# Gated DeltaNet layer of a two-layer trunk: later transfers of the block inverses in ScalarE's program, a pinned order of GpSimd's chain, and another PSUM rotation for two heads

## The chip, the cores and the metric

The kernel runs on one core of one Trainium2 chip. The metric is the device time of one execution in microseconds (us); the trace is that of one execution, recorded by the hardware profiler. Names of engines below: PE is TensorE (matmuls), ACT is ScalarE, DVE is VectorE, POOL is GpSimd, SP is the engine that issues most DMAs. Each of the five runs its own list of instructions strictly one after the other, and waits on semaphores for what the other engines produce. ACT also issues DMAs; such an issue stands in its list like any other instruction.

## The reference

The input is 512 tokens of width 1024. Two layers are computed, each as FFN (SwiGLU), mixer, FFN, all with residual adds. Layer 0 has an attention mixer, layer 1 a gated DeltaNet mixer with 8 heads of width 128. The change is in the second mixer only, which is in short (the reference uses chunks of 64 tokens, the kernel blocks of 128):

```python
q, k, v = silu(conv4(h @ w_in))            # per head; q and k are l2-normalized
beta, g = sigmoid(..), -exp(a_log) * softplus(..)
gc      = cumsum(g)                        # inside a chunk
l_mat   = strict_lower((k * beta) @ k.T * decay)
t_mat   = inverse(I + l_mat)               # triangular solve per chunk
u, w    = t_mat @ (v * beta), t_mat @ (k * beta * exp(gc))
a_qk    = lower(q @ k.T * decay)
for each chunk:                            # a scan over a 128 x 128 state
    v_new = u - w @ state
    o     = (q * exp(gc)) @ state + a_qk @ v_new
    state = state * exp(gc_last) + (k * exp(gc_last - gc)).T @ v_new
out = (rms_norm(o) * silu(gate)) @ w_out
```

## The kernel before

**Projections.** All large matmuls are done three times on rounded parts (high times high, low times high, high times low). A panel of weights comes by a DMA of SP into `raw`, ACT makes the high part `wh` (L174), DVE the low part `wl` (L175). One projection (queries, keys, values or gate of one pair of heads) fills two PSUM buffers `mm`, one for each head, with 96 matmuls of 0.23 us in two half panels. There are only these two `mm` buffers: the next projection starts when DVE has read the one before into `cx` (L926 in `gdn_conv`). A convolution of four taps follows: the first tap on ACT (`cy`, L929), three on DVE (`cy`, L931), an activation on ACT (`c`, L934 or L937), for most of the first two pairs' projections one more pass on DVE (`c`, L935).

**The delta rule.** Heads go in four pairs, 0 to 3. A pair passes through stages: `prep` (`gdn_keys`: transposes of k in PSUM buffers `pa`; row norms; `kdec` by ACT; then `pl`, the products k k^T, of which DVE makes `iu`, the matrix to be inverted; then q k^T, of which DVE makes `aq` in the tile `du`), `base` (`gdn_base`, below), `turned` (values turned and scaled, `vb`), `scan` (`gdn_head`, two heads side by side) and `gated`. Heads 0 and 1 are pair 0, heads 4 and 5 pair 2. PSUM has three buffers `pa` and three `pb`.

**`gdn_base`** inverts the 32x32 diagonal blocks of both heads of a pair at once. ACT issues two DMAs `iud<-iu` to DRAM and four `lb<-iud` back, which lay the blocks out over 128 partitions. POOL then runs a chain of 31 steps of two instructions each (`tmp<-rr,lb`, `rr<-rr,tmp`), 62 in all. After it ACT issues four DMAs `rd<-rr` to DRAM (L1043) and two `r<-rd` back (L1046), one for each head. In `gdn_head`, DVE transposes r into t (L1055), and PE begins the scan with `pb<-t,iu`. At its end DVE computes `a` from the output's squares (L1129), POOL raises it to the power -1/2 (`rs<-a`, L160), ACT scales the output by it (`on<-on,rs`, L1133), and PE transposes the output in `gated` (`pa<-ident,on`, L99).

**What sets the order.** `blend` runs one stream of projections (the filler: queries 0, values 0, keys 1, queries 1, values 1, gate 0, keys 2, queries 2, values 2, gate 1, out 0, keys 3, ..., out 2; a step is three matmuls) against the stages, by the table PLAN: a stage's first step and its pitch, both in filler steps. PE is held to the order in which this program is traced. On ACT, DVE and POOL a scheduler of the compiler orders the instructions, by its own estimate of times. `keep_in_program_order` (here `pin`) adds the constraint that an instruction comes behind the instruction of the same engine that was traced immediately before it. Each chain step of POOL is one step of its stage.

Of the kernel before, what the change touches and what calls it, by code (L numbers as in the profile page):

```python
# [13 lines left out]
ALU = mybir.AluOpType  # L14
# [21 lines left out]
QD = 5  # L36
NHID = 14
HDPAD, HIDPAD = 112, 0
TANH = ((0, 0), (2, 0), (1, 1), (0, 1))
PLAN = (  # L40
    ("setup", 0, 3.5, 5), ("decays", 0, 22, 0), ("prep", 0, 25.5, 2.1), ("turned", 0, 43.5, 1.82),
    ("base", 0, 51.5, 0.45), ("decays", 1, 47.5, 4.52), ("decays", 2, 57.5, 3.84),
    ("decays", 3, 50.5, 1.87), ("prep", 1, 82.5, 4.2), ("base", 1, 99.5, 0.41),
    ("scan", 0, 91.5, 1.91), ("turned", 1, 134.5, 1.09), ("gated", 0, 152.5, 1.33),
    ("scan", 1, 138.5, 2), ("prep", 2, 136.5, 3), ("base", 2, 151.5, 0.65),
    ("turned", 2, 192.5, 0.85), ("gated", 1, 188.5, 1.26), ("scan", 2, 202.5, 2.3),
    ("prep", 3, 209.5, 2.42), ("base", 3, 245.5, 0.47), ("turned", 3, 254.5, 0.85),
    ("gated", 2, 251.5, 0.73), ("scan", 3, 260.5, 0.95), ("gated", 3, 283.5, 1.22),
# [53 lines left out]
class Trunk:  # L102
# [610 lines left out]
    def odd_mixer(self, gain, w_in, conv, a_log, dt_bias, gnorm, w_out):  # L713
        nc = self.nc
        H = 8
        self.prenorm(gain)
        with ExitStack() as st:
            pool = st.enter_context(self.tc.tile_pool(name="gdn", bufs=2))
            one = st.enter_context(self.tc.tile_pool(name="gdn1", bufs=1))
            self.te = Ordered(self.tc)  # L720
            half = one.tile([P, 96], F32, name="half")
            nc.vector.tensor_scalar(half, conv, 0.5, None, ALU.mult)
            n = H // 2
            Ks = [[{}, {}] for _ in range(n)]
            keys, queries, values = (
                lambda p, sec=sec: self.gdn_proj(pool, Ks[p], sec, p, w_in, conv, half)
                for sec in (1, 0, 2))
            gate = lambda p: self.gdn_gate(pool, Ks[p], p, w_in)
            out = lambda p, mk=(self.mm_ps, self.mm_ps): self.gdn_out(Ks[p], p, w_out, mk)
            prep = lambda p: side_by_side(*(self.gdn_keys(pool, G, 2 * p + j, K)  # L730
                                            for j, K in enumerate(Ks[p])))
            base = lambda p: self.gdn_base(pool, G, Ks[p])
            turned = lambda p: (self.gdn_values(pool, K) for K in Ks[p])
            scan = lambda p: side_by_side(*(self.gdn_head(pool, G, 2 * p + j, K)
                                            for j, K in enumerate(Ks[p])))
            gated = lambda p: (self.gdn_gated(pool, K, gnorm) for K in Ks[p])
# [210 lines left out]
    def gdn_keys(self, pool, G, h, K):  # L947

        nc = self.nc
        S, big, v3, rep = self.gdn_tools(pool)
        du, kT, qT = G["du"][h], K["k"], K["q"]
        small = lambda tag: pool.tile([P, NB], F32, tag=tag, name=tag, bufs=4)
        pk = self.a_ps()
        for b in range(NB):
            self.te.transpose(out=pk[:, S[b]], in_=kT[:, S[b]], identity=self.ident)
        sk, br, kd = small("sk"), small("br"), small("kd")
        for b in range(NB):  # L960
            sq = pool.tile([P, P], F32, tag="gosq", name="gosq", bufs=1)
            nc.scalar.activation(sq, pk[:, S[b]], AF.Square, accum_out=sk[:, b:b + 1])
        nc.vector.tensor_scalar(sk, sk, 1e-6, None, ALU.add)
        nc.vector.reciprocal(br, sk)
        vs = small("vs")
        self.rpow(vs, sk, NB, 0.5)
        nc.vector.tensor_tensor(br, br, G["bt"][:, :, h], op=ALU.mult)
        nc.vector.tensor_tensor(kd, br, G["kdc"][:, :, h], op=ALU.mult)
        K["vs"] = vs
        kdec = big("kdec", bufs=4)  # L970
        for b in range(NB):
            nc.scalar.activation(kdec[:, S[b]], pk[:, S[b]], AF.Copy, scale=kd[:, b:b + 1])
# [12 lines left out]
        pq = self.b_ps()
        for b in range(NB):
            self.te.matmul(pq[:, S[b]], lhsT=kT[:, S[b]], rhs=qT[:, S[b]], start=b == 0, stop=b == 3)
        aq = du
        for b in range(NB):
            G["last"] = nc.vector.scalar_tensor_tensor(  # L990
                aq[:, S[b]], pq[:, S[b]], br[:, b:b + 1], du[:, S[b]], ALU.mult, ALU.mult)
        yield
        yield

        pn = self.a_ps()
        for b in range(NB):
            self.te.transpose(out=pn[:, S[b]], in_=qT[:, S[b]], identity=self.ident)
        sn = small("sn")
        for b in range(NB):
            sq = pool.tile([P, P], F32, tag="gosq", name="gosq", bufs=1)  # L1000
            nc.scalar.activation(sq, pn[:, S[b]], AF.Square, accum_out=sn[:, b:b + 1])
        eq = small("eq")
        nc.vector.tensor_scalar(eq, sn, P * EPS, 1e-6 * P * EPS, ALU.mult, ALU.add)
        K.update(aq=aq, eq=eq)
# [10 lines left out]
            nc.scalar.activation(vb[:, S[b]], pv[:, S[b]], AF.Copy, scale=K["vs"][:, b:b + 1])  # L1015
        K["vb"] = vb

    def gdn_base(self, pool, G, Ks):


        nc = self.nc
        n = BASE
        iud = self.dram.tile([2 * HPITCH], F32, tag="iud", name="iud", bufs=2)
        for j, K in enumerate(Ks):
            nc.scalar.dma_start(self.rows_of(iud, j), K["iu"].rearrange("p (t s) -> p t s", s=P))
        lb = pool.tile([P, n, n], F32, tag="lb", name="lb", bufs=1)
        rr = pool.tile([P, n // 4, n], F32, tag="rr", name="rr", bufs=1)
        tmp = pool.tile([P, 9 * n], F32, tag="tmp", name="tmp", bufs=1)
        quarters = [slice(q * 2 * NBLK, (q + 1) * 2 * NBLK) for q in range(4)]
        for s in quarters:  # L1030
            nc.scalar.dma_start(lb[s], self.blocks_of(iud))
        nc.scalar.copy(out=rr, in_=G["eye"])
        for j in range(n - 1):
            m, k = n - 1 - j, j // 4 + 1
            sh = [P, k, m]
            p = tmp[:, :k * m].rearrange("p (a b) -> p a b", b=m)
            nc.gpsimd.tensor_tensor(p, rr[:, :k, j:j + 1].broadcast_to(sh),  # L1037
                                    lb[:, j, j + 1:].rearrange("p (o m) -> p o m", o=1)
                                    .broadcast_to(sh), op=ALU.mult)
            nc.gpsimd.tensor_tensor(rr[:, :k, j + 1:], rr[:, :k, j + 1:], p, op=ALU.subtract)  # L1040
            yield
        for q, s in enumerate(quarters):
            nc.scalar.dma_start(self.blocks_of(G["rd"], q, 4), rr[s])  # L1043
        for j, K in enumerate(Ks):
            K["r"] = pool.tile([P, T], F32, tag="r", name="r", bufs=3)
            nc.scalar.dma_start(K["r"].rearrange("p (t s) -> p t s", s=P), self.rows_of(G["rd"], j))  # L1046
        yield
# [156 lines left out]
```

## Time and profile before

| what | us |
|---|---|
| three runs | 2032.43, 2032.97, 2032.87 |
| their median | 2032.87 |
| the profiled execution's own time | 2032.96 |
| span of its instructions | 2031.2 |
| PE busy in it | 1999.0 |
| DVE, ACT, POOL busy | 1084.6, 748.3, 130.9 |

The span is the time between the first and the last instruction; what lies around it is 1.8 us. A busy share says nothing yet of who waits for whom; that is read from the waits and from the order of rows on each engine.

### The profile page before, as it was taken

To read this page: it belongs to the slowest core of one execution; us is meant where nothing else is said; L and a number is where in the kernel's file an instruction comes from. 1 tells how busy PE (TensorE), PEld (TensorE's weight loads), DVE (VectorE), ACT (ScalarE), POOL (GpSimd) and SP (SyncE) were. 2 spreads that over 40 slices of the span, in tenths; PEclk is the share of its full clock that TensorE was granted. 3 is DMA by queue.
4 is the path that set the end of the run, shared out by engine and by line. 5 is a ranking of instruction groups with operands and counts; after the bars stand their busy time and mean duration, and the time that the engine had idled before them with its cause. 6 is when DMAs were issued, how large, how long until landed. Compare 5 with 4: busy or idle time off the path is not lost.

```text
span 2031.2 us, 24843 instructions
## 1 busy us (share of the span) xinstructions
PE 1999.0 (98%) x9786; PEld 1667.5 (82%) x9786; DVE 1084.6 (53%) x1752; ACT 748.3 (37%) x1359; POOL 130.9 (6%) x298
## 2 busy tenths in 40 slices
PE   8999999999999999999999999998999999999998
PEld 7888888889888888888888888877877788888887
DVE  6452454597675433444544344478577685443543
ACT  5232233355663222233332232355465453322322
POOL 0000000100000000000000000005432400000000
PEclk9999999999999999999999999999999999999999
DMA  4333333222123333333333333234223233223332
GB/s 157 94 99 98 94 99 98 86 84 73 47 90 103 94 104 94 94 103 94 94 95 102 94 95 103 93 111 115 77 80 92 75 100 104 94 90 97 93 101 76
DMA packets 189866, 192.24 MB, mean 95 GB/s; under 512 B 28546, under 2 KB 165044, under 8 KB 189748
## 3 DMA queue, kind: packets, MB, share of 16 engines
q1 hardware_dynamic: 158916, 182.62, 28.7%
q10 hardware_dynamic: 30832, 8.02, 1.7%
q8 instruction: 77, 1.26, 0.3%
q14 instruction: 41, 0.34, 0.1%
HBM read 185.35 MB, written 5.26 MB: 94 GB/s over the span
## 4 chain that ended last, share of the span: by engine, by line
PE 89%; POOL 5%; DMA 2%; DVE 1%; issue 1%; ACT 1%; ACTq 0%; SPq 0%; POOLq 0%
PE mm L181 10%; PE mm L182 10%; PE mm L183 10%; PE pa L181 9%; PE pa L183 8%; PE pa L182 8%; PE pb L181 8%; PE pb L183 8%; PE pb L182 8%; PE mm L96 4%; POOL tmp L1037 2%; POOL rr L1040 2%; PE pb L96 1%; DMA lb<-iud 1%; DMA iud<-iu 1%
## 5 line engine op out<-in xcount | busy, mean ns | idle before, releaser
L175 DVE TENSOR_TENSOR wl<-raw,wh 128x1024 fp32r<-128x1024 f32 (+1 forms) x348 | 413.2, 1187 | 564.1 <-ACT wh L174 563.1
L174 ACT CAST wh<-raw 128x1024 fp32r<-128x1024 f32 (+1 forms) x348 | 355.6, 1022 | 702.0 <-PE pb L182 279.9
L181 PE MATMUL mm<-xnh,wh 128*128 128x512 f32 (+1 forms) x816 | 316.5, 389 | 0.6 <-ACT wh L174 0.6
L183 PE MATMUL mm<-xnh,wl 128*128 128x512 f32 (+1 forms) x816 | 317.1, 389 | 0.0
L182 PE MATMUL mm<-xnl,wh 128*128 128x512 f32 (+1 forms) x816 | 316.7, 388 | 0.0
L181 PEld LDWEIGHTS mm<-xnh,wh 128*128 128x128 f32 x816 | 154.3, 189 | 31.6 <-ACT wh L174 1.0
L183 PEld LDWEIGHTS mm<-xnh,wl 128*128 128x128 f32 x816 | 154.2, 189 | 30.5 <-issue 0.5
L182 PEld LDWEIGHTS mm<-xnl,wh 128*128 128x128 f32 x816 | 154.3, 189 | 30.4 <-issue 0.2
L181 PE MATMUL pa<-xnh,wh 128*128 128x512 f32 x400 | 156.2, 390 | 0.0
L183 PE MATMUL pa<-xnh,wl 128*128 128x512 f32 x400 | 155.8, 389 | 0.0
L183 PE MATMUL pb<-xnh,wl 128*128 128x512 f32 x400 | 155.7, 389 | 0.0
L181 PE MATMUL pb<-xnh,wh 128*128 128x512 f32 x400 | 155.7, 389 | 0.0
L182 PE MATMUL pa<-xnl,wh 128*128 128x512 f32 x400 | 155.7, 389 | 0.0
L182 PE MATMUL pb<-xnl,wh 128*128 128x512 f32 x400 | 155.7, 389 | 0.0
L226 ACT CAST hid<-hd 128x512 fp32r<-128x512 f32 x88 | 54.5, 620 | 209.0 <-DVE hd L398 209.0
L96 PE MATMUL mm<-xnh,wh 128*128 128x512 f32 x256 | 109.2, 426 | 12.0 <-DVE cx L926 12.0
L392 DVE TENSOR_TENSOR gr<-mm,rb 128x512 f32<-128x512 f32 x80 | 55.2, 691 | 94.7 <-PE mm L183 94.6
L183 PE MATMUL pb<-hid,wl 128*128 128x512 f32 x264 | 102.8, 389 | 0.0
L181 PE MATMUL pa<-hid,wh 128*128 128x512 f32 x264 | 102.7, 389 | 0.0
L182 PE MATMUL pa<-hid,wh 128*128 128x512 f32 x264 | 102.7, 389 | 0.0
L183 PE MATMUL pa<-hid,wl 128*128 128x512 f32 x264 | 102.7, 389 | 0.0
L181 PE MATMUL pb<-hid,wh 128*128 128x512 f32 x264 | 102.7, 389 | 0.0
(308 smaller groups left out, 3365.1 us busy)
## 6 DMA issues: line engine op xcount, KB each, us to landing
raw<-in_ffn_w_gate_dram SPq DMA_DIRECT2D x88, 512.0 KB, 3.6
raw<-in_ffn_w_up_dram SPq DMA_DIRECT2D x88, 512.0 KB, 3.6
raw<-in_ffn_w_down_dram SPq DMA_DIRECT2D x88, 512.0 KB, 3.6
raw<-in_gdn_w_in_dram SPq DMA_DIRECT2D x32, 512.0 KB, 3.9
raw<-in_att_w_in_dram SPq DMA_DIRECT2D x24, 512.0 KB, 3.5
raw<-in_gdn_w_out_dram SPq DMA_DIRECT2D x16, 256.0 KB, 2.7
xr<-in_x_dram SPq DMA_DIRECT2D x4, 512.0 KB, 5.6
raw<-in_att_w_out_dram SPq DMA_DIRECT2D x4, 512.0 KB, 3.4
```

The lines of the kernel that those rows point to most:

```text
L96: return self.tc.keep_in_program_order(self.engine.matmul(*args, **kw))
L174: nc.scalar.copy(out=h[:, :n], in_=raw[:, :n])
L175: nc.vector.tensor_tensor(l[:, :n], raw[:, :n], h[:, :n].bitcast(F32), op=ALU.subtract)
L181: self.te.matmul(out, lhsT=lh, rhs=rh, start=start, stop=False)
L182: self.te.matmul(out, lhsT=lh, rhs=rl, start=False, stop=False)
L183: self.te.matmul(out, lhsT=ll, rhs=rh, start=False, stop=stop)
L226: nc.scalar.copy(out=h, in_=src)
L392: nc.vector.tensor_tensor(gr, g[j], self.rb, op=ALU.mult)
L1037: nc.gpsimd.tensor_tensor(p, rr[:, :k, j:j + 1].broadcast_to(sh), lb[:, j, j + 1:].rearrange("p (o m) -> p o m", o=1) .broadcast_to(sh), o ...
L1040: nc.gpsimd.tensor_tensor(rr[:, :k, j + 1:], rr[:, :k, j + 1:], p, op=ALU.subtract)
```

## The change

Four edits. First, 36 empty steps (50 for pair 1, none for pairs 2 and 3) stand between the chain's last step and the issues `rd<-rr`, and those issues are pinned. Second, both instructions of each chain step on POOL are pinned. Third, `pl` of heads 0 and 1 takes a buffer `pb` instead of `pa`. Fourth, PLAN starts scans 0 and 1 three filler steps later.

```diff
+WAIT = 36, 50, 0, 0
 PLAN = (
...
-    ("scan", 0, 91.5, 1.91), ("turned", 1, 134.5, 1.09), ("gated", 0, 152.5, 1.33),
-    ("scan", 1, 138.5, 2), ("prep", 2, 136.5, 3), ("base", 2, 151.5, 0.65),
+    ("scan", 0, 94.5, 1.91), ("turned", 1, 134.5, 1.09), ("gated", 0, 152.5, 1.33),
+    ("scan", 1, 141.5, 2), ("prep", 2, 136.5, 3), ("base", 2, 151.5, 0.65),
...
-        pl = self.a_ps()
+        pl = self.b_ps() if h < 2 else self.a_ps()
...
-            nc.gpsimd.tensor_tensor(rr[:, :k, j + 1:], rr[:, :k, j + 1:], p, op=ALU.subtract)
+            pin(nc.gpsimd.tensor_tensor(p, rr[:, :k, j:j + 1].broadcast_to(sh),
+                                        lb[:, j, j + 1:].rearrange("p (o m) -> p o m", o=1)
+                                        .broadcast_to(sh), op=ALU.mult))
+            pin(nc.gpsimd.tensor_tensor(rr[:, :k, j + 1:], rr[:, :k, j + 1:], p, op=ALU.subtract))
             yield
+        yield from [None] * wait
         for q, s in enumerate(quarters):
-            nc.scalar.dma_start(self.blocks_of(G["rd"], q, 4), rr[s])
+            pin(nc.scalar.dma_start(self.blocks_of(G["rd"], q, 4), rr[s]))
```

The compiled programs show where instructions move. Line numbers of the changed kernel are higher by one to two. The first place is POOL's list in the chain of pair 3 (`rr_13054`); `rs_13070` and `rs_13078` belong to the two heads of pair 2, and `vs` to pair 3's values. Before, the chain begins, and ends, like this:

```order
L160 TENSOR_TENSOR vs_12664<-sk_12651,halfTrue_89 128x4
L1037 TENSOR_TENSOR tmp_13055<-rr_13054,lb_13053 128x31
L1040 TENSOR_TENSOR rr_13054<-rr_13054,tmp_13055 128x31
L1037 TENSOR_TENSOR tmp_13055<-rr_13054,lb_13053 128x30
...
L1037 TENSOR_TENSOR tmp_13055<-rr_13054,lb_13053 128x16
L160 TENSOR_TENSOR rs_13070<-a2_13068,halfFalse_87 128x4
L1040 TENSOR_TENSOR rr_13054<-rr_13054,tmp_13055 128x8x2
L160 TENSOR_TENSOR rs_13078<-a2_13076,halfFalse_87 128x4
L1037 TENSOR_TENSOR tmp_13055<-rr_13054,lb_13053 128x8
```

In the changed program the same chain begins like this:

```order
L161 TENSOR_TENSOR vs_12664<-sk_12651,halfTrue_89 128x4
L1038 TENSOR_TENSOR tmp_13055<-rr_13054,lb_13053 128x31
L1041 TENSOR_TENSOR rr_13054<-rr_13054,tmp_13055 128x31
L1038 TENSOR_TENSOR tmp_13055<-rr_13054,lb_13053 128x30
L1041 TENSOR_TENSOR rr_13054<-rr_13054,tmp_13055 128x30
L161 TENSOR_TENSOR rs_13070<-a2_13068,halfFalse_87 128x4
L161 TENSOR_TENSOR rs_13078<-a2_13076,halfFalse_87 128x4
L1038 TENSOR_TENSOR tmp_13055<-rr_13054,lb_13053 128x29
```

Both `rs` of pair 2 moved from the chain's end to a place behind its second step: 58 chain instructions now stand behind them. Elsewhere POOL's list is as before.

The second place is ACT's list around `rd<-rr` of pair 0. `c_10842` and `c_10853` are pair 1's queries, `cx_10933` and `cx_10943` (changed: `cx_10925`) pair 1's values. Before:

```order
L929 ACTIVATE cy_10848<-cx_10845,half_10034 128x512
L174 CAST wh_11041<-raw_11039 128x1024
L934 ACTIVATE c_10842<-cy_10837 128x512
L1043 DMA rd_10279<-rr_10687 32x8x32 x4
L929 ACTIVATE cy_10936<-cx_10933,conv_248 128x512
L934 ACTIVATE c_10853<-cy_10848 128x512
L174 CAST wh_11161<-raw_11159 128x1024
L1046 DMA r_10881<-rd_10279 128x4x128
```

In the changed program:

```order
L930 ACTIVATE cy_10837<-cx_10834,half_10034 128x512
L175 CAST wh_10949<-raw_10947 128x1024
L1045 DMA rd_10279<-rr_10687 32x8x32 x3
L930 ACTIVATE cy_10848<-cx_10845,half_10034 128x512
L1045 DMA rd_10279<-rr_10687 32x8x32
L935 ACTIVATE c_10842<-cy_10837 128x512
L1048 DMA r_10963<-rd_10279 128x4x128
...
L175 CAST wh_11041<-raw_11039 128x1024
L935 ACTIVATE c_10853<-cy_10848 128x512
```

Against the projections' work, the first `rd` issues moved forward: they stand ahead of `cy_10848`, `c_10842` and the cast `wh_11041`, behind which they stood. For pair 1 they moved back, from a place ahead of the values' `cy` to one behind all eight `on<-on,rs` of pair 0.

The third place is DVE's list at the end of pair 1's values, where t is made from r of pair 0 and `cx` empties the two buffers `mm`. Before:

```order
L926 TENSOR_TENSOR cx_10933<-mm_10856,rb_10133 128x512
L931 SCALAR_TENSOR_TENSOR cy_10848<-cx_10845,half_10034,cy_10848 128x512
...
L931 SCALAR_TENSOR_TENSOR cy_10936<-cx_10933,conv_248,cy_10936 128x512
L926 TENSOR_TENSOR cx_10943<-mm_10857,rb_10133 128x512
...
L175 TENSOR_TENSOR wl_11162<-raw_11159,wh_11161 128x1024
L1055 STREAM_TRANSPOSE t_11057<-r_10881 128x512
```

In the changed program:

```order
L1057 STREAM_TRANSPOSE t_11066<-r_10963 128x512
L932 SCALAR_TENSOR_TENSOR cy_10848<-cx_10845,half_10034,cy_10848 128x512
L176 TENSOR_TENSOR wl_11042<-raw_11039,wh_11041 128x1024
L926 MEMSET cx_10935 128x3
L936 SCALAR_TENSOR_TENSOR c_10853<-c_10853,cy_10848 128x512
L1057 STREAM_TRANSPOSE t_11068<-r_10965 128x512
L927 TENSOR_TENSOR cx_10925<-mm_10856,rb_10133 128x512
L932 SCALAR_TENSOR_TENSOR cy_10928<-cx_10925,conv_248,cy_10928 128x512
L927 TENSOR_TENSOR cx_10935<-mm_10857,rb_10133 128x512
```

Both transposes moved ahead of the two `cx`, behind which they stood.

## Rows read from the trace of the kernel before

**Rows 1.** The page, first part: busy time, share of span, instructions.

```profile
PE 1999.0 (98%) x9786; PEld 1667.5 (82%) x9786; DVE 1084.6 (53%) x1752; ACT 748.3 (37%) x1359; POOL 130.9 (6%) x298
```

**Rows 2.** Waits of PE in the second mixer: us in total, times, longest.

```profile
PE mm L96 <- DVE cx L926: 12.0, 3, 6.5
```

**Rows 3.** Busy time per 50 us stretch; behind the engines granted clock, DMA share, GB/s.

```profile
1400.00:1450.00 50.00, 43.00 (x303) 35.71 (x302) 29.69 (x70) 22.17 (x62) 19.19 (x48) 0.93 0.38 98
```

**Rows 4.** Timeline of PE: start, duration, instruction, idle time before and its releaser.

```profile
1368.61 1.16 PE L96 MATMUL pa<-c 128*128 128x128 f32 x8 [2.56 <-ACT kdec L972]
...
1386.90 0.39 PE L96 MATMUL mm<-xnh,wh 128*128 128x512 f32 x1
...
1406.92 0.39 PE L96 MATMUL mm<-xnh,wh 128*128 128x512 f32 x1
...
1417.20 0.80 PE L96 MATMUL mm<-xnh,wh 128*128 128x512 f32 x1 [6.49 <-DVE cx L926]
...
1422.36 0.40 PE L96 MATMUL mm<-xnh,wh 128*128 128x512 f32 x1
...
1475.59 0.80 PE L96 MATMUL mm<-xnh,wh 128*128 128x512 f32 x1 [4.82 <-DVE cx L926]
...
1479.60 0.91 PE L99 MATMUL pa<-ident,c 128*128 128x128 f32 x4
...
1605.88 1.35 PE L99 MATMUL pa<-ident,on 128*128 128x128 f32 x4 [2.54 <-ACT on L1133]
...
1616.70 0.89 PE L96 MATMUL pb<-t,iu 32*32 32x32 f32 x32
```

**Rows 5.** Timeline of ACT around the transfers of pairs 0 and 1.

```profile
1413.12 1.82 ACTq L1043 DMA_DIRECT2D rd<-rr  x4
1415.04 0.72 ACT L929 ACTIVATE cy<-cx,conv 128x512 f32<-128x512 f32 x1 [11.99 <-issue]
...
1470.39 1.81 ACTq L1043 DMA_DIRECT2D rd<-rr  x4
```

**Rows 6.** Timeline of DVE at the places that the change reorders.

```profile
1370.47 0.74 DVE L931 SCALAR_TENSOR_TENSOR cy<-cx,half,cy 128x512 f32<-128x512 f32 x1
...
1385.17 0.68 DVE L926 TENSOR_TENSOR cx<-mm,rb 128x512 f32<-128x512 f32 x1
...
1416.46 0.68 DVE L926 TENSOR_TENSOR cx<-mm,rb 128x512 f32<-128x512 f32 x1
1417.06 0.68 DVE L935 SCALAR_TENSOR_TENSOR c<-c,cy 128x512 f32<-128x512 f32 x1
1417.66 0.75 DVE L931 SCALAR_TENSOR_TENSOR cy<-cx,conv,cy 128x512 f32<-128x512 f32 x1
1418.32 1.22 DVE L175 TENSOR_TENSOR wl<-raw,wh 128x1024 fp32r<-128x1024 f32 x1
1419.46 0.70 DVE L1055 STREAM_TRANSPOSE t<-r 128x512 f32<-128x512 f32 x1
...
1599.91 0.15 DVE L1129 SCALAR_TENSOR_TENSOR a<-gss,eq 128x4 f32<-128x4 f32 x1
```

**Rows 7.** Timeline of POOL: chain of pair 0, chain of pair 3.

```profile
1381.34 0.24 POOL L1037 TENSOR_TENSOR tmp<-rr,lb 128x31 f32<-128x31 f32 x1 [14.08 <-DMA lb<-iud]
...
1412.88 0.21 POOL L1040 TENSOR_TENSOR rr<-rr,tmp 128x8 f32<-128x8 f32 x1
...
1579.70 0.56 POOL L1037 TENSOR_TENSOR tmp<-rr,lb 128x31 f32<-128x31 f32 x1 [14.28 <-DMA lb<-iud]
...
1581.85 0.57 POOL L1037 TENSOR_TENSOR tmp<-rr,lb 128x29 f32<-128x29 f32 x1
...
1604.38 1.01 POOL L160 TENSOR_TENSOR rs<-a,halfFalse 128x4 f32<-128x4 f32 x1
1605.36 0.22 POOL L1040 TENSOR_TENSOR rr<-rr,tmp 128x16 f32<-128x16 f32 x1
...
1606.80 0.21 POOL L1040 TENSOR_TENSOR rr<-rr,tmp 128x8 f32<-128x8 f32 x1
```

More of the change, by code (lines that the diff above doesn't have):

```diff
@@ L731, in odd_mixer @@
                                             for j, K in enumerate(Ks[p])))
-            base = lambda p: self.gdn_base(pool, G, Ks[p])
+            base = lambda p: self.gdn_base(pool, G, Ks[p], WAIT[p])
             turned = lambda p: (self.gdn_values(pool, K) for K in Ks[p])
@@ L1016, in gdn_values, with gdn_base @@
         K["vb"] = vb
-    def gdn_base(self, pool, G, Ks):
-        nc = self.nc
+    def gdn_base(self, pool, G, Ks, wait):
+        nc, pin = self.nc, self.tc.keep_in_program_order
         n = BASE
@@ L1036, in gdn_base @@
             p = tmp[:, :k * m].rearrange("p (a b) -> p a b", b=m)
-            nc.gpsimd.tensor_tensor(p, rr[:, :k, j:j + 1].broadcast_to(sh),
-                                    lb[:, j, j + 1:].rearrange("p (o m) -> p o m", o=1)
-                                    .broadcast_to(sh), op=ALU.mult)
-            nc.gpsimd.tensor_tensor(rr[:, :k, j + 1:], rr[:, :k, j + 1:], p, op=ALU.subtract)
+            pin(nc.gpsimd.tensor_tensor(p, rr[:, :k, j:j + 1].broadcast_to(sh),
+                                        lb[:, j, j + 1:].rearrange("p (o m) -> p o m", o=1)
+                                        .broadcast_to(sh), op=ALU.mult))
+            pin(nc.gpsimd.tensor_tensor(rr[:, :k, j + 1:], rr[:, :k, j + 1:], p, op=ALU.subtract))
             yield
+        yield from [None] * wait
         for q, s in enumerate(quarters):
-            nc.scalar.dma_start(self.blocks_of(G["rd"], q, 4), rr[s])
+            pin(nc.scalar.dma_start(self.blocks_of(G["rd"], q, 4), rr[s]))
         for j, K in enumerate(Ks):
```

## The prediction

> **What bounds the kernel now.** I first read the page's busy times: PE works 98% of the span [rows 1], so time can only come or go where PE stands idle or runs slowly. Next I read what PE waits for in the second mixer [rows 2]: 12.0 us in all for `cx`. PE's timeline [rows 4] has the single waits: 2.56 us for `kdec`, because `pl` wants a buffer `pa`; 6.49 and 4.82 for `cx`; 2.54 for `on`. Behind the last three, matmuls of one weight panel start 0.43 us apart rather than 0.23 us; in the stretch that holds the first one the granted clock is 0.93 on average [rows 3], so part of it ran at the lower of TensorE's two levels, 1.2 GHz. From 1417.20 to 1422.36 twelve matmuls take 5.16 us, where 12 x 0.23 = 2.8 would do: 2.4 us lost. From 1475.59 to 1479.60 nine take 4.01 rather than 2.07: 1.9 lost. I take 2 us for the third.
>
> Why do the two long waits for `cx` end so late? ACT stands at `rd<-rr` until POOL's chain has ended: 11.99 us lie idle ahead of its next `cy`, the issue included [rows 5]. POOL's last instruction of pair 0 ends at 1412.88 + 0.21 = 1413.09, and `rd` goes out at 1413.12 [rows 5, 7]; behind it come `cy`, DVE's `cy`, DVE's `cx` at 1416.46 [rows 6], and PE at 1417.20. Pair 1 repeats this at 1470.39. The third wait is one for POOL too: `rs` of pair 2 stands at the end of pair 3's chain and runs at 1604.38 [rows 7], although its second `a` was there at 1599.91 + 0.15 = 1600.06 [rows 6].
>
> **Pair 3, the largest term.** POOL's new list puts both `rs` of pair 2 behind the second chain step of pair 3. The chain starts at 1579.70 and begins its third step at 1581.85 [rows 7]; from now on it must stand there for `a`, which is made at the end of scan 2, at 1600.06. The wait is no more than a move in the list, but 58 chain instructions are queued behind it, for these ACT's `rd`, for that DVE's t, and for that PE's scan 3. Worked out on before's time axis:
> - The first `rs` can go at 1599.4, the second at 1600.4, as they take 0.98 from one start to the next (1604.38 to 1605.36) [rows 7]; the chain goes on at 1601.4.
> - Its remaining part took from 1581.85 to 1606.80 + 0.21 = 1607.01, or 25.2 us, in which the two `rs` cost about 1.7 (0.98 each, less some 0.13 by which each starts early). That leaves 23.5. Some of these instructions took twice as long as their neighbours; they may gain up to 2.3 us where DVE is idle. I take 22.6, between 21.2 and 23.5. End: 1624.0.
> - From a chain's end to the first t took 1419.46 - 1413.09 = 6.4, and a transpose 0.70 [rows 6, 7]: PE can start `pb<-t,iu` at 1631.1. It started it at 1616.70 [rows 4].
>
> So scan 3 starts 14.4 us later, bounds 13 to 16. This already uses up what the earlier `rs` saves: the wait of 2.54 and its slow matmuls go, so PE arrives near 1616.7 - 2.5 - 2.0 = 1612.2, and then stands 18.9 us. Scan 3 and out 3 depend on it and the filler ahead of it is spent, so nothing gives this back.
>
> Behind the new wait the clock has to rise again. The rows give 1.9 to 2.4 us for waits of 4.82 and 6.49; a line through the two reaches 2.4 + 12.4 x 0.3 = 6.1 at 18.9. I take 2, because the slow matmuls run at one level, start 0.43 us apart after either wait, and the price hardly depends on the wait. The Trainium skill (TensorE: Matmul & The Clock Gate, What's actually happening) says that the gate knows only two states, half and full rate, and that it turns on recent activity; by that a longer wait is no slower behind than a shorter one, and the sum stays at 2 rather than 6 us. The trace agrees as far as waits up to 6.49 us show it.
>
> **Pair 0.** What goes: 2.56 at `pl`, since `pb` is free there. But DVE is dense there. In the new list, between the `cy` of 1370.47 and the `cx` of keys 1's second head stand 7 `cy`, 2 `c`, 1 `cx`, 1 `wl`, 4 `iu`, 8 `aq`, 24 `du` and small ones, 18.3 to 19.4 us by their starts in this trace. This `cx` is then done at about 1390 rather than 1385.17 + 0.68 = 1385.9 [rows 6]. PE wanted that buffer for the second half of queries 1 at 1386.90 [rows 4], wants it 2.6 us earlier now and gets it at 1390.5: it stands 6.2 us and is 3.6 late; with 2 us at the lower clock, less a wait of 0.7 that goes, values 1 end at about 1411.8, not at 1406.9 [rows 4].
>
> Next, gate 0 needs the two `mm`. Their `cx` now stand behind both t<-r on DVE, so behind POOL's chain. I put the chain's end at 1411.6: it starts near 1381.9 and takes 29.7, between pair 0's 31.75 (1381.34 to 1413.09) and pair 3's 25.6 (27.3 less its `rs`) [rows 7], nearer to the first. From there to the first `cx` I add what the rows show as time between starts: 6.4 to t, 0.6 t, 0.7 `cy`, 1.1 `wl`, 0.6 `c`, 0.6 t, and the `cx`'s 0.68 [rows 6]: 10.7. PE begins gate 0 at 1422.3, not at 1406.9 [rows 4]: a new wait of 10.5 us in place of 6.49. Its first 24 matmuls take 5.5 + 2.4 = 7.9 to 8.4, up to 1430.5; before, that point was 1422.36 [rows 4]. Pair 0 is 8.2 us later, though the `rd` were meant to go later: on ACT they stand earlier among the projections' work. Bounds: -5, if DVE's new order costs PE nothing and only half of the second wait comes, and +11, if the chain ends at 1413.5.
>
> **Pair 1.** The wait of 4.82, 1.9 at the lower clock and a small wait of 0.5 go, 7.2 in all, as ACT's held place now lies behind more of the projections. What is late next: `rd` stands behind all eight `on<-on,rs`, so r comes later and PE waits about 2.3 at scan 1, in spite of its later start; and `pl` of head 4 or 5 meets `iu` late on DVE, 0 to 3.4; I take 3.3. Net -1.6, bounds -7 and +2. Pair 2 I cost at nothing: its chain, transfers and `rs` of pair 1 stand in one order with the others as before.
>
> **Sum.** 8.2 - 1.6 + 14.4 + 2.0 = +23.0 on the profiled execution's own 2032.96 (span 2031.2 and 1.8 around it; the median of the runs is 0.09 lower): **2056.0 us**.
>
> **The rivals.**
> - *Early parts even.* DVE and ACT find slack that my sum of starts denies them, and pairs 0 and 1 cost as much as they return: 2032.96 + 16.4 = 2049.4. For it: ACT is busy only 22 of 50 us there [rows 3]. Against it: t and `cx` stand on DVE in an order that slack does not change.
> - *Early waits vanish.* -2.56 - 6.49 - 2.4 - 4.82 - 1.9 = -18.2, against +16.4 in pair 3: 2031.2, even or a little faster. This is what the change would do if the two held transfers no longer delayed `cx`. Against it: the list of DVE at pair 1's values.
> - *Faster: the earlier `rs` pays.* If the chain of pair 3 still ended in time, pair 2's `on` would leave 3 us earlier, the wait of 2.54 and 2.0 at the lower clock would go, and with even early parts this gives 2028.5. It decides at 1612.2: the chain must end by 1612.2 - 7.1 = 1605.1, so `a` would have to be there by about 1581, 19 us before it is. Only a scan 2 that runs far ahead of the chain brings that about; I see none.
> - *Slower at the clock.* 6 instead of 2 us behind the long wait, and the upper bound in pair 0: 2056 + 4 + 3 = 2063.
>
> **How the numbers follow.** The forecast (loss in pair 0, long wait in pair 3) has 0.58, with its own range 2051 to 2062; early parts even 0.27 (2042 to 2051); early waits vanish 0.06; the earlier `rs` pays 0.05; above 2062 0.04. From 2042 to 2062 I leave out about 0.17. What a measurement of this kernel can tell from no change is 0.2%, or 4.1 us. Faster by more: the fourth case and a part of the third, 0.07. Within: the rest of the third, 0.05. Slower: 0.88.
>
> **What would show it.** In the changed kernel's trace POOL should stand some 18 us between the second and third step of pair 3's chain, released by DVE's `a`, and PE should stand 15 to 20 us ahead of `pb<-t,iu` of scan 3; the wait for `on` at `pa<-ident,on` should be gone, and the one for `kdec` too. Around pair 1's values PE should stand about 10 us for `cx`, with DVE's t<-r just ahead of that `cx`. No wait of 4.8 us for `cx` should follow in pair 1, but short ones for t and `iu`. I am wrong if POOL meets `a` ready, if DVE reaches `cx` without standing at r, or if PE has work between that I take for spent.

## The result and the profile after

The changed kernel takes 2066.57 us (median of 6 runs, 2065.35 to 2067.22) against 2032.65 (6 runs, 2031.37 to 2033.69): a ratio of 1.0167, interval 1.0154 to 1.018, or 33.9 us slower. The forecast was 2056.0 with a range of its own from 2051 to 2062: the time lies 10.6 us above the forecast and 4.6 above the range. The direction and the largest place, pair 3, were right; other terms were not, above all the price of the clock.

The profiled execution of after has a span of 2063.6 us, 32.4 more than before; rows and sums below are those of one execution each. Its waits of PE in the second mixer, in the columns of [rows 2]:

```profile
PE pb L97 <- DVE t L1057: 19.8, 2, 19.6
PE mm L97 <- DVE cx L927: 11.0, 1, 11.0
PE pa L100 <- DVE c L936: 5.1, 2, 4.5
PE pa L97 <- DVE iu L983: 3.4, 1, 3.4
PE pa L100 <- ACT on L1135: 2.3, 1, 2.3
```

Of the 12.0 us for `cx` one wait of 11.0 is left, and a wait of 19.6 us for t is new. PE's timeline has the single ones, as in [rows 4]:

```profile
1383.74 1.11 PE L100 MATMUL pa<-ident,c 128*128 128x128 f32 x4 [4.51 <-DVE c L936]
...
1420.72 0.77 PE L97 MATMUL mm<-xnh,wh 128*128 128x512 f32 x1 [11.05 <-DVE cx L927]
...
1498.70 1.65 PE L97 MATMUL pa<-c 128*128 128x128 f32 x6 [3.40 <-DVE iu L983]
...
1548.10 1.35 PE L100 MATMUL pa<-ident,on 128*128 128x128 f32 x4 [2.26 <-ACT on L1135]
...
1642.90 1.65 PE L97 MATMUL pb<-t,iu 32*32 32x32 f32 x32 [19.61 <-DVE t L1057]
...
1649.44 1.97 PE L97 MATMUL pb<-t,iu 64*64 64x64 f32 x16
```

The last row is 1.07 to 1.14 us long at full clock. The same matmul of PE can be found in both traces by the number of matmuls ahead of it, and the difference of its two starts shows how late after is. Ahead of the second mixer, where the programs are alike, this difference is -1.33 (1295.22 and 1293.90): the profiled execution of after was that much ahead. It is taken off below.

| up to this matmul | start before | start after | added here | forecast |
|---|---|---|---|---|
| ahead of scan 0 (pair 0) | 1425.80 | 1432.81 | +8.3 | +8.2 |
| ahead of pair 1's `on` (pair 1) | 1535.66 | 1544.32 | +1.7 | -1.6 |
| behind it (pair 2's part) | 1542.09 | 1552.74 | +2.0 | 0 |
| first `pb<-t,iu` of scan 3 (pair 3) | 1616.70 | 1642.90 | +15.5 | +14.4 |
| end of the second mixer (clock) | 1659.93 | 1692.34 | +6.2 | +2.0 |
| sum | | | +33.7 | +23.0 |

POOL's timeline shows why scan 3 is late (compare [rows 7]):

```profile
1592.20 0.26 POOL L1041 TENSOR_TENSOR rr<-rr,tmp 128x30 f32<-128x30 f32 x1
1610.05 1.99 POOL L161 TENSOR_TENSOR rs<-a,halfFalse 128x4 f32<-128x4 f32 x2 [17.59 <-DVE a L1131]
1612.01 0.24 POOL L1038 TENSOR_TENSOR tmp<-rr,lb 128x29 f32<-128x29 f32 x1
...
1616.40 1.27 POOL L1038 TENSOR_TENSOR tmp<-rr,lb 128x48 f32<-128x48 f32 x1
...
1635.84 0.21 POOL L1041 TENSOR_TENSOR rr<-rr,tmp 128x8 f32<-128x8 f32 x1
```

POOL stands 17.59 us between the second and the third step of the chain, released by DVE's `a`: the row that the prediction asked for. The chain ends at 1635.84 + 0.21 = 1636.05, and DVE makes t 6.1 us later:

```profile
1642.13 1.49 DVE L1057 STREAM_TRANSPOSE t<-r 128x512 f32<-128x512 f32 x2 [21.52 <-DMA r<-rd]
```

At pair 1's values DVE stands as forecast, with both t<-r ahead of the first `cx`, which comes at 1419.92:

```profile
1416.28 0.71 DVE L1057 STREAM_TRANSPOSE t<-r 128x512 f32<-128x512 f32 x1 [1.86 <-DMA r<-rd]
...
1419.29 0.71 DVE L1057 STREAM_TRANSPOSE t<-r 128x512 f32<-128x512 f32 x1
1419.92 0.65 DVE L927 TENSOR_TENSOR cx<-mm,rb 128x512 f32<-128x512 f32 x1
```

The windows of after (columns as in [rows 3]) show the clock: in the 14.5 us behind the long wait PE has work without a gap, 14.50 of 14.50, and is granted 0.50, the level of 1.2 GHz, all the time; then 1.00. Behind the wait of 3.40 for `iu` it is 0.50 too. The last line is from before, where PE comes to scan 3 without a wait: there the same matmuls, 14.54 of 14.70 us busy, run at 1.00, the level of 2.4 GHz.

```profile
1643.00:1657.50 14.50, 14.50 (x129) 11.51 (x130) 4.34 (x12) 2.37 (x7) 0.00 (x0) 0.50 0.07 20
1658.00:1668.00 10.00, 9.84 (x63) 8.39 (x62) 6.07 (x18) 3.92 (x15) 0.00 (x0) 1.00 0.01 2
1498.70:1504.00 5.30, 5.30 (x21) 4.26 (x22) 1.86 (x7) 1.66 (x5) 0.00 (x0) 0.50 0.33 100
```

```profile
1616.70:1631.40 14.70, 14.54 (x168) 12.10 (x168) 6.72 (x20) 4.01 (x14) 0.00 (x0) 1.00 0.13 38
```

Two corrections to the text ahead of the prediction. A projection has 48 matmuls, 24 in each half panel, not 96; the prediction reckoned with 24. And the `cy` that stood behind pair 1's `rd` belongs to the queries of pair 2, not to values: `rd` goes out at 1470.39, and the values of pair 2 are then still being multiplied.

### The profile page after: what moved, and what is told of

The parts are those of the page before. It is cut to its first block, busy times and chain, and to the rows that moved or that the text cites. A ratio compares the mean times of both kernels' runs of the same rounds, so it can differ in the third digit from the quotient of the medians.

```text
span 2063.6 us, 24852 instructions
## 1 busy us (share of the span) xinstructions
PE 2005.2 (97%) x9786; PEld 1671.5 (81%) x9786; DVE 1084.4 (53%) x1752; ACT 746.7 (36%) x1359; POOL 132.8 (6%) x298
## 4 chain that ended last, share of the span: by engine, by line
PE 88%; POOL 5%; DMA 3%; DVE 2%; issue 1%; ACT 1%; ACTq 0%; SPq 0%; POOLq 0%; DVEq 0%
PE mm L183 10%; PE mm L182 10%; PE mm L184 10%; PE pa L182 8%; PE pa L184 8%; PE pa L183 8%; PE pb L182 8%; PE pb L184 8%; PE pb L183 8%; PE mm L97 4%; POOL rr L1041 2%; POOL tmp L1038 2%; PE pb L97 1%; DMA r<-rd 1%; DMA lb<-iud 1%
## 5 line engine op out<-in xcount | busy, mean ns | idle before, releaser
L97 PE MATMUL mm<-xnh,wl 128*128 128x512 f32 x256 | 103.1, 403 | 0.0
L97 PE MATMUL mm<-xnl,wh 128*128 128x512 f32 x256 | 103.0, 403 | 0.0
```

Of the source, the lines that this page charges most:

```text
L97: return self.tc.keep_in_program_order(self.engine.matmul(*args, **kw))
```

## The experiments

The main theory: three edits have effects of their own. The pins on POOL cost by pair 3 alone, through `a`; `pl` in `pb` turns DVE's order at pair 0 and costs there; the pinned `rd` and the empty steps cost nothing. The rival for the first: the pins cost at the other pairs too, or the wait at scan 3 comes from the later `rd`. Each ratio below is against the kernel before, measured beside it (medians 2032.3 to 2032.7).

**e1_unpin3**: after, with the chain of pair 3 alone unpinned.

```diff
+PINNED = (0, 1, 2)
...
+        hold = pin if pinned else lambda ins: ins
...
-            pin(nc.gpsimd.tensor_tensor(rr[:, :k, j + 1:], rr[:, :k, j + 1:], p, op=ALU.subtract))
+            hold(nc.gpsimd.tensor_tensor(rr[:, :k, j + 1:], rr[:, :k, j + 1:], p, op=ALU.subtract))
```

> The changed kernel with one thing undone: the chain of pair 3 on POOL is not pinned (pairs 0 to 2 still are), and both rs of pair 2 stand at that chain's end again. Theory (the pin of pair 3's chain costs 15.9 us at scan 3 and 6.2 us at the lower clock behind it): 2066.6 - 22.1 = 2044.5 us, between 2042 and 2047, no wait of PE near 20 us ahead of scan 3, and the wait for on at pa<-ident,on back at about 2.5 us. Rival (the wait at scan 3 comes from the later iu and lb of pair 3, not from the pin): 2064 to 2068, with the wait of some 20 us still there.

Measured: 2042.34, ratio 1.005 (1.0035 to 1.0065). The wait at scan 3 is gone, and that of 2.54 for `on` is back ahead of it; `cx` and `iu` stay:

```profile
PE mm L98 <- DVE cx L928: 12.3, 1, 12.3
PE pa L101 <- DVE c L937: 5.7, 2, 5.1
PE pa L98 <- DVE iu L984: 3.4, 1, 3.4
PE pa L101 <- ACT on L1137: 2.5, 1, 2.5
```

Without the pins of this one chain 24.2 of the 33.9 us come back: by the table above 21.7 of it at scan 3 and in the clock behind it, and most of the rest at pair 1's `on`, for which PE does not wait here.

**e2_poolpins**: before, with the pins on both instructions of each step in all four chains and nothing else.

```diff
...
+            pin(nc.gpsimd.tensor_tensor(rr[:, :k, j + 1:], rr[:, :k, j + 1:], p, op=ALU.subtract))
```

> The kernel before with one thing added: all chain instructions on POOL pinned, no empty steps, no pin on rd, pl in pa, PLAN as before. In the lists of the engines only the two rs of pair 2 move, and what hangs on them. Theory: 2032.7 + 22 = 2054.7 us, between 2051 and 2058, a wait of 18 to 20 us ahead of scan 3, the three older waits unchanged. Rival (with the earlier parts of before, POOL meets a sooner and the pin is nearly free or saves the wait of 2.5 us): 2028 to 2034.

Measured: 2054.19, ratio 1.0105 (1.0089 to 1.0122), +21.5 us, with the same wait:

```profile
1633.96 1.65 PE L97 MATMUL pb<-t,iu 32*32 32x32 f32 x32 [19.57 <-DVE t L1057]
```

So the wait needs neither the later `rd` nor the late pairs 0 and 1. In POOL's list only the two `rs` of pair 2 change their place against before, so the pins on the other three chains move nothing there.

**e3_rd**: before, with the empty steps and the pinned `rd` alone.

```diff
+WAIT = 36, 50, 0, 0
...
+        yield from [None] * wait
...
-            nc.scalar.dma_start(self.blocks_of(G["rd"], q, 4), rr[s])
+            pin(nc.scalar.dma_start(self.blocks_of(G["rd"], q, 4), rr[s]))
```

> The kernel before with the empty steps (36, 50) and the pinned rd alone. Theory (the empty steps and pins move nothing at pair 0 and little at pair 1, where two rd now stand behind one cy): 2030 to 2035 us, the wait of 6.5 us for cx at pair 0 unchanged. Rival (the pinned rd are what delays pair 0, by holding ACT earlier): 2039 to 2043, with a wait near 11 us for cx.

Measured: 2032.2 (10 runs), ratio 1.0000 (0.9991 to 1.0009). At pair 0 the wait for `cx` is 6.14, hardly other than 6.49 [rows 4], and `rd` stands in ACT's list where it stood, between a `c` (1401.83) and the values' `cy` (1414.10). At pair 1 the wait for `cx` stays too: 4.95 for 4.82. A pin ties `rd` only to the instruction of ACT traced just before it; it does not say what `rd` should stand behind.

**e4_pl**: before, with `pl` of heads 0 and 1 in `pb` alone.

```diff
-        pl = self.a_ps()
+        pl = self.b_ps() if h < 2 else self.a_ps()
```

> The kernel before with pl of heads 0 and 1 in a buffer pb alone. Theory (this edit alone turns the order on DVE and ACT around at pair 0: rd earlier, t ahead of cx): 2032.7 + 8.5 = 2041 us, between 2037 and 2044, waits of 4 to 6 us for c near 1380 us and near 11 us for cx, none for kdec. Rival (the freed pl saves its wait of 2.56 us and does nothing else): 2029 to 2031.

Measured: 2039.78, ratio 1.0038 (1.0023 to 1.0053), +7.1 us. The wait for `kdec` goes, and those of pair 0 come. PE's timeline, and DVE's behind it:

```profile
1384.38 0.82 PE L101 MATMUL pa<-ident,c 128*128 128x128 f32 x4 [4.54 <-DVE c L937]
...
1419.59 0.77 PE L98 MATMUL mm<-xnh,wh 128*128 128x512 f32 x1 [9.22 <-DVE cx L928]
```

```profile
1415.68 1.43 DVE L1059 STREAM_TRANSPOSE t<-r 128x512 f32<-128x512 f32 x2
...
1418.75 1.28 DVE L928 TENSOR_TENSOR cx<-mm,rb 128x512 f32<-128x512 f32 x2
```

This edit alone moves both t<-r ahead of the two `cx`, and `rd` forward on ACT. The loss at pair 0, which reads like a matter of the transfers, comes from the PSUM rotation.

**e9_after_pa**: after, with `pl` back in `pa`, as the counterpart.

```diff
-        pl = self.b_ps() if h < 2 else self.a_ps()
+        pl = self.a_ps()
```

> The changed kernel with pl of heads 0 and 1 back in a buffer pa; pins, empty steps and later scans stay. Theory (the parts add up: the pins of pair 3 cost 21.5, pl 7.1, the rest little): 2066.6 - 7 to 9 = 2058 to 2060 us or, if the later scans also cost by themselves nothing, down to 2055; the waits for c near 1380 us gone, the wait for cx at pair 0 back at about 6.5 us. Rival (the empty steps and later scans bring pair 0's loss as well, once POOL is pinned): 2064 to 2068.

Measured: 2058.06, ratio 1.0127 (1.0112 to 1.0142), 8.5 us under after; the wait for `cx` falls from 11.05 to 5.71 and that at scan 3 stays at 19.51. All five times lie where the theory had them.

Next the clock, the term that failed worst. Theory W: how long the clock stays low is set by the work that follows the wait, and is much the same behind a short and a long one. Rival L: it is set by the length of the wait, as the line through [rows 4] had it. Two kernels vary the wait by the step of the chain behind which `rs` stands.

**e5_rs21** and **e6_rs15**: before, with pair 3's chain pinned and traced faster, so that `rs` of pair 2 comes behind step 21, or 15 (in after: 2).

```diff
+PINNED = (3,)
...
-    ("prep", 3, 209.5, 2.42), ("base", 3, 245.5, 0.47), ("turned", 3, 254.5, 0.85),
+    ("prep", 3, 209.5, 2.42), ("base", 3, 245.5, 0.034), ("turned", 3, 254.5, 0.85),
```

(e6_rs15 has 0.05 instead of 0.034.)

> The kernel before, with the chain of pair 3 alone pinned and its steps traced 0.034 instead of 0.47 filler steps apart, so that both rs of pair 2 stand behind step 21 of the chain (before: near its end; changed kernel: behind step 2). From the trace of before: POOL stands from 1597.4 to 1599.4 for a, the chain ends at 1609.4 instead of 1607.0, t is ready at 1616.5, and PE, which loses its wait of 2.5 us and 2.0 at the lower clock, arrives at 1612.2 and waits 4.3 us there. Theory W (what PE does behind a wait sets how long the clock stays low: the scan's small matmuls keep it low for some 14 us, at a cost of 6 us, however short the wait): 2032.7 - 4.5 + 4.3 + 6 = 2038.5 us. Theory L (a wait of 4 us costs 2 us at the lower clock as the waits of 2.5 to 6.5 us did): 2034.5 us, low clock for 4 to 5 us behind the wait.

> As the one before, but the steps 0.05 apart, so that the rs stand behind step 15. POOL stands from 1592.1 to 1599.4, the chain ends at 1614.6, t is ready at 1621.7, PE waits 9.5 us. Theory W: 2032.7 - 4.5 + 9.5 + 6 = 2043.7 us, and a low clock for some 14 us behind the wait. Theory L (cost grows with the wait): 2.4 to 3.3 us at the lower clock, 2040 to 2041 us.

Measured: 2041.01, ratio 1.0043 (1.0028 to 1.0058), and 2043.61, ratio 1.0056 (1.0041 to 1.0071). PE's wait and the windows of e5_rs21:

```profile
1617.22 1.64 PE L98 MATMUL pb<-t,iu 32*32 32x32 f32 x32 [5.17 <-DVE t L1059]
```

```profile
1612.00:1617.00 5.00, 0.05 (x1) 0.00 (x0) 0.55 (x1) 0.62 (x2) 0.00 (x0) 1.00 0.47 122
1617.00:1634.00 17.00, 16.78 (x137) 13.46 (x138) 5.23 (x15) 2.37 (x7) 0.00 (x0) 0.50 0.06 18
1634.00:1644.00 10.00, 9.84 (x60) 8.37 (x59) 6.36 (x19) 3.96 (x15) 0.00 (x0) 1.00 0.04 13
```

and of e6_rs15, whose wait is 9.98:

```profile
1622.00:1637.00 15.00, 14.79 (x130) 11.77 (x131) 4.72 (x13) 2.37 (x7) 0.00 (x0) 0.50 0.06 19
```

A wait of 5.17 us leaves the clock low for 17 us, one of 9.98 for 15, one of 19.61 (after) for 14.6. L, which had 4 to 5 us low behind the short wait, is refuted. W came within 0.1 us for e6_rs15 and was 2.5 short for e5_rs21, about half of it because the low clock cost 7.2 rather than 6 (table below); PE's wait was 5.17 rather than 4.3.

**e7_dense**: e2_poolpins with 16 wide matmuls of t and `iu`, whose result nobody uses, between the wait and the scan (32 records in the trace).

```diff
+DENSE = 16
...
+        if h == 6:
+            px = self.b_ps()
+            for i in range(DENSE):
+                b = i % NB
+                self.te.matmul(px, lhsT=t[:, S[b]], rhs=iu, start=True, stop=True)
```

> The kernel before with all chain instructions on POOL pinned (a wait near 20 us ahead of scan 3, as measured at 2054.2 us), and 16 extra matmuls of 128x512 that read t of head 6 put right behind the wait, ahead of the scan's first matmul; their result is not used. Theory W: dense matmuls bring the clock back within 4 to 6 us of their start, so the scan runs at 2.4 GHz, and the total is 2054.2 plus the block's time less up to 4 us. Theory L (a wait of 20 us leaves the clock low for some 14 us, whatever comes): the granted clock stays at half until 14 to 15 us behind the wait's end.

Measured: 2065.87 (2 runs), ratio 1.0166 (1.0145 to 1.0186), 11.7 us above e2_poolpins, though the scan begins only at 1649.52, 17.7 us behind the wait's end: the added block, and three matmuls of the filler that stood ahead of the wait before. PE's timeline and windows:

```profile
1631.86 17.03 PE L98 MATMUL pb<-iu,t 128*128 128x512 f32 x32 [20.42 <-DVE t L1058]
...
1653.47 1.14 PE L98 MATMUL pb<-t,iu 64*64 64x64 f32 x16
```

```profile
1632.00:1638.00 6.00, 6.00 (x8) 2.36 (x9) 0.57 (x1) 0.00 (x0) 0.00 (x0) 0.50 0.01 3
1638.00:1650.00 12.00, 12.00 (x51) 5.61 (x50) 0.00 (x0) 0.00 (x0) 0.00 (x0) 1.00 0.00 0
```

Behind the longest wait of all the clock is back in some 6 us, and the scan runs at full speed: its 64x64 matmuls take 1.14 rather than 1.97 us. 17.7 - 11.7 = 6.0 us is about what the low clock had cost the scan. The same shows without a difference of medians. From scan 3's first matmul to the first one behind the second mixer PE runs the same matmuls in every kernel:

| kernel | PE's wait at scan 3 | first matmul | behind the mixer | between | more than before |
|---|---|---|---|---|---|
| before | none | 1616.70 | 1659.93 | 43.2 | |
| e11_pool_queue_noshift (below) | 1.22 | 1619.69 | 1670.12 | 50.4 | 7.2, with the wait |
| e5_rs21 | 5.17 | 1617.22 | 1667.64 | 50.4 | 7.2 |
| e6_rs15 | 9.98 | 1622.21 | 1671.67 | 49.5 | 6.2 |
| e2_poolpins | 19.57 | 1633.96 | 1684.25 | 50.3 | 7.1 |
| after | 19.61 | 1642.90 | 1692.34 | 49.4 | 6.2 |
| e7_dense | 20.42 | 1649.52 | 1692.73 | 43.2 | 0.0 |

(In e11 the wait falls behind the scan's first matmuls and is in the sum: 6.0 without it.) The price does not follow the wait's length: it is 6 to 7 us behind waits from 1.22 to 19.61 us, and nothing where wide matmuls had brought the clock back first.

The last four kernels ask whether the transfers can be kept out of the way of `cx` as the change set out to, and so beat both kernels. The theory: at full effect the waits of 6.49 and 4.82 go with their slow matmuls. The rival: ACT's or POOL's list then stands elsewhere.

**e8_rd_behind_cy**: before, empty steps and later scans as in after, no pins on POOL, `pl` in `pa`; `rd` is tied behind the `cy` of the second head of the projection whose `cx` PE waits for (values 1 for pair 0, queries 2 for pair 1).

```diff
+AFTER = {0: (2, 3), 1: (0, 5)}
...
-            nc.scalar.dma_start(self.blocks_of(G["rd"], q, 4), rr[s])
+            with self.tc.issue_after(self.cy[AFTER[h0]]) if h0 in AFTER else nullcontext():
+                nc.scalar.dma_start(self.blocks_of(G["rd"], q, 4), rr[s])
```

> The kernel before with the empty steps (36, 50), scans 0 and 1 three steps later, and the four rd of pairs 0 and 1 queued on ACT behind the cy of the second head of the projection whose cx PE waits for (values of pair 1, queries of pair 2), in place of a pin to whatever was traced last. No pin on POOL, pl in pa. Theory (the waits of 6.49 and 4.82 us come only from ACT standing at rd ahead of that cy): both go, with 4.3 us at the lower clock, and up to 2 us come back at the start of scan 0 and 1: 2032.7 - 15.6 + 2 = 2019 us, between 2017 and 2024. Rival (PE then waits for t at scan 0 and 1 as long as it did for cx): 2029 to 2035.

Measured: 2029.63 (10 runs), ratio 0.9984 (0.9975 to 0.9994): 3 us under before, and the fastest kernel here, but far from the 2019 of the theory. Both waits for `cx` are gone, but PE has new ones. Its timeline:

```profile
1424.80 2.08 PE L99 MATMUL pa<-c 128*128 128x128 f32 x8 [4.79 <-ACT kdec L975]
...
1476.56 0.66 PE L102 MATMUL pa<-ident,c 128*128 128x128 f32 x4 [2.22 <-ACT vb L1018]
```

and that of ACT, where the work for `kdec` now stands behind the four `rd`:

```profile
1416.20 1.82 ACTq L1049 DMA_DIRECT2D rd<-rr  x4
1418.06 0.28 ACT L965 ACTIVATE gosq<-pa 128x128 f32<-128x128 f32 x1 [8.18 <-issue]
```

The standing of ACT is moved, not removed. The time is the rival's, by another wait than it named.

**e12_cy_pl**: e8_rd_behind_cy with `pl` of heads 2 and 3 in `pb`, against the wait for `kdec`.

```diff
-        pl = self.a_ps()
+        pl = self.b_ps() if 2 <= h < 4 else self.a_ps()
```

> As e8_rd_behind_cy (rd queued behind cy; 2029.6 us, with a new wait of 4.8 us for kdec because pl of head 2 or 3 wants a buffer pa), with pl of heads 2 and 3 in pb. Theory (that wait is one for the buffer alone): it goes, with up to 3 us at the lower clock: 2022 to 2026 us. Rival (PE then waits at the same place for br or kd, which stand behind rd on ACT too): 2029 to 2032.

Measured: 2030.42 (10 runs), ratio 0.9989 (0.9979 to 0.9998). In place of `kdec` PE waits 4.61 us for `gosq`, which stands in the same queue behind `rd`: the rival's time. No gain over e8_rd_behind_cy.

**e10_pool_queue** and **e11_pool_queue_noshift**: before, with `rd` and r issued by POOL, with the scans three steps later and without.

```diff
-            nc.scalar.dma_start(self.blocks_of(G["rd"], q, 4), rr[s])
+            nc.gpsimd.dma_start(self.blocks_of(G["rd"], q, 4), rr[s])
...
-            nc.scalar.dma_start(K["r"].rearrange("p (t s) -> p t s", s=P), self.rows_of(G["rd"], j))
+            nc.gpsimd.dma_start(K["r"].rearrange("p (t s) -> p t s", s=P), self.rows_of(G["rd"], j))
```

> The kernel before, with scans 0 and 1 three steps later and all rd and r transfers issued by POOL itself, behind its chain, in place of ACT. No pins, no empty steps, pl in pa. Theory (ACT no longer stands at rd, so cx, gosq and kdec of the next projection are free, and the six issues cost POOL a few us that only t feels): the waits of 6.49 and 4.82 us for cx go, with 4.3 us at the lower clock, PE waits up to 5 us for t at scan 0: 2018 to 2026 us. Rival (issue by POOL is so slow, or its transfers so late, that PE waits for t at scans 0, 1 and 3 as long as it did for cx): 2030 to 2040.

> As e10_pool_queue, with scans 0 and 1 where they were before. Theory: t of pair 0 is ready no sooner, so what the waits for cx give back turns into a wait for t at scan 0 of 4 to 7 us, followed by the scan's small matmuls at the lower clock: 2024 to 2031 us, some us above e10_pool_queue. Rival (t is ready in time anyway): within 2 us of e10_pool_queue.

Measured: 2044.44 (4 runs, 2043.28 to 2050.44), ratio 1.0065 (1.0046 to 1.0085), and 2038.87 (5 runs, 2035.84 to 2043.5), ratio 1.0035 (1.0021 to 1.0049). Both expectations fell, theories and rivals. In e10_pool_queue PE waits 9.21 us for `kdec` and 7.2 for `vb`, both of ACT. ACT stands even without the issues, since the next pair's `rr` is made by ACT in a buffer that `rd` must have read, and POOL's issue takes longer than ACT's 1.82 [rows 5]:

```profile
1428.57 2.08 PE L98 MATMUL pa<-c 128*128 128x128 f32 x8 [9.21 <-ACT kdec L974]
```

```profile
1419.18 0.40 ACT L1035 COPY rr<-eye 128x256 f32<-128x256 f32 x1 [11.38 <-DMA rd<-rr]
```

```profile
1415.25 2.56 POOL L1047 DMA_DIRECT2D rd<-rr  x4 [0.40 <-POOL rr L1043]
```

In e11_pool_queue_noshift PE stands 6.56 us ahead of scan 0, where the expectation put 4 to 7, and 8.5 more for `vb`, which it did not have. Its trace, taken from the slowest of the five runs, also shows the smallest wait with the full price of the clock. The second head's t comes 1.22 us late at scan 3, and the clock, still 1.00 there, is low for the next 13.6 us:

```profile
1621.49 0.59 PE L98 MATMUL pb<-t,iu 32*32 32x32 f32 x16 [1.22 <-DVE t L1059]
```

```profile
1622.20:1635.80 13.60, 13.60 (x99) 10.50 (x99) 3.19 (x9) 2.37 (x7) 0.00 (x0) 0.50 0.06 20
```

## Why the prediction was right in direction and short in size

The 10.7 us between the sums of the table are 4.2 at the clock behind the long wait, 3.3 at pair 1, 2.0 at pair 2, 1.1 at pair 3 and 0.1 at pair 0. With the clock priced as measured the forecast would have been 2060.2, inside its range.

**Pair 3, mechanism right, 1.1 us short.** e1_unpin3 and e2_poolpins show it from both sides: 24.2 and 21.5 us with the low clock behind it. Worked out by the prediction's own steps on the rows of after: `rs` runs when `a` is there and the chain goes on 1.3 us after the second `a`, as forecast; the rest of the chain takes 1636.05 - 1612.01 = 24.0 us, where I took 22.6 and set the upper bound at 23.5; from there to t it is 6.1 for 6.4. I had let the chain gain where DVE is idle. But DVE works until 1620.6 (its t at 1642.13 comes behind 21.52 us of idle time), and until then single instructions of the chain take up to 1.3 us (the row at 1616.40), later none above 0.35.

**The clock behind the long wait, the step that failed.** I took 2 us "because the slow matmuls run at one level, start 0.43 us apart after either wait, and the price hardly depends on the wait". That much holds: the windows show 0.50 and 1.00, and at scan 3 the price is much the same behind 1.22 us as behind 19.61. The Trainium skill (TensorE: Matmul & The Clock Gate, What's actually happening) has two states, and the windows agree. What failed is the step from there to 2 us: that price was measured ahead of panels of 128x512 matmuls [rows 4] and was carried over to a scan. The price is the time at the lower level. Behind scan 3's wait come 32x32 and 64x64 matmuls with groups of three wide ones between them, and the level stays low for 14.6 us: +6.2 rather than +2.0. e7_dense shows that the work decides: with wide matmuls first the price at the scan is gone. The line that I had rejected gave 6.1, the right number by a wrong reason, as e5_rs21 shows. The rival "slower at the clock" had 6 for this term, and this half of it came; its other half, the upper bound at pair 0, did not.

**Pair 0, right.** +8.3 against +8.2: the wait for `c` near 1384 is 4.5 (I had 6.2, for `cx`), that for `cx` 11.05 (10.5). The miss at the first wait does not show in the sum, since the second one's end is set by the chain and DVE: PE goes on at 1420.72 + 1.33 = 1422.05, forecast 1422.3. The cause stated there was incomplete: e3_rd and e4_pl show that the new list comes from `pl` in `pb` alone, 7.1 of it, and not from the edit on `rd`.

**Pair 1, wrong sign.** The wait of 4.82, its slow matmuls and the small wait go, and `iu` costs 3.40 (3.3 forecast). But I gave this new wait no clock of its own: PE works 5.30 us at 0.50 behind it, by my estimate up to 2.6 lost. Waits of 0.7 for `vb` and 0.5 inside the scan, and 0.8 in scan 0, take what the smaller wait for t (0.2, not 2.3) saved. These rows make +1.0; the other 0.7 I cannot assign. So +1.7 rather than -1.6. Which edit moves pair 1's wait can be read across the kernels: the pins on POOL (e2_poolpins, 5.21), the empty steps with the pinned `rd` (e3_rd, 4.95) and `pl` (e4_pl, 5.22) each leave the wait for `cx` in place; it is gone, and that for `iu` there, in after, e1_unpin3 and e9_after_pa, which join the later scans to the pinned `rd`.

**Pair 2, not nothing.** I took its lists for unchanged, and DVE's is not. Before, both `a` of pair 1 stand ahead of pair 2's two t<-r:

```profile
1536.39 0.16 DVE L1129 SCALAR_TENSOR_TENSOR a<-gss,eq 128x4 f32<-128x4 f32 x1 [0.20 <-ACT gosr L1125]
...
1537.66 1.50 DVE L1055 STREAM_TRANSPOSE t<-r 128x512 f32<-128x512 f32 x2 [1.11 <-DMA r<-rd]
```

In after the first t<-r stands ahead of both, so `a`, and POOL's `rs` behind it, wait for a transfer that they do not need, and PE waits 2.26 for pair 1's `on`:

```profile
1545.77 0.71 DVE L1057 STREAM_TRANSPOSE t<-r 128x512 f32<-128x512 f32 x1 [2.70 <-DMA r<-rd]
1546.40 0.19 DVE L1131 SCALAR_TENSOR_TENSOR a<-gss,eq 128x4 f32<-128x4 f32 x2
```

```profile
1546.60 1.99 POOL L161 TENSOR_TENSOR rs<-a,halfFalse 128x4 f32<-128x4 f32 x2 [10.32 <-DVE a L1131]
```

ACT had finished the squares for these `a` at 1543.68. That this transfer sets the wait is read from the rows, not tested. The new order stands in e1_unpin3 and e9_after_pa too; the wait comes and goes with the transfer: e1_unpin3, where r is 0.40 late, has none here, e9_after_pa 1.77. It also bears on the sum over edits: 21.5 (e2_poolpins) and 9.6 (e1_unpin3) make 31.1 of the 33.9; the other 2.8 may be this wait, but are not clear of the intervals.

The waits of 4.82, 2.54 (at scan 3) and 2.56 went as foretold, and the short ones for `iu` came. The rivals with even early parts, with the early waits gone or with the earlier `rs` paying did not occur. What stays open: the later scans were not run alone. e10_pool_queue with them is 5.6 us above e11_pool_queue_noshift, but in kernels with other waits, and their runs scatter by 7 us. A place for `rd` that holds up neither `cx` nor `kdec` was not found.

## What to carry to other kernels

Before pinning the order of a list, look at which foreign instruction the pin puts in the middle of a chain, and when its input is there: here two `rs` of 1 us each held 58 instructions for 17.6 us. Price a new wait of PE with the work that follows it: here 6 to 7 us stood behind waits of 1.2 to 20 us ahead of a scan, and 2.4 behind one of 6.49 ahead of a panel. A buffer taken from another rotation can change the order of the engines that empty it: here one `pl` cost 7.1 us that way. An issue that waits for its data is better tied behind a named instruction than to whatever was traced before it, and what then stands behind it has to be looked at too (e8_rd_behind_cy).

## What the hardware showed that was not expected

With PE busy all the time in both, the granted clock stayed at 0.50 for 14.6 us in after's scan of small matmuls, and for some 6 us in e7_dense's 128x512 ones. The same scan ran at 1.00 in before, so small matmuls did not lower the clock by themselves; behind a wait they did not soon raise it. A shorter wait was not cheaper: 13.6 us low behind 1.22, 17 behind 5.17 (where the clock was still 1.00 in the wait and fell as the work began), 15 behind 9.98, 14.6 behind 19.61. What the chip looks for cannot be told from these runs. Four issues of DMAs took POOL 2.56 us and ACT 1.82.
